# The output stage of a decoder block by seven products: another order of the products, sums stored from ScalarE's queue, no arithmetic on GpSimd

## The chip, the cores and the metric

The kernel runs on one core of one Trainium2 chip. The time is that of the whole program on the device, in microseconds. A core has TensorE (PE, matmul), VectorE (DVE), ScalarE (ACT), GpSimd (POOL) and SyncE (SP). Each engine runs its own instructions in the order in which they are written for it, and waits on semaphores for the others. SP, ACT and POOL also start DMAs from their queues.

## The reference, cut to what matters

A block of a decoder: a norm, one projection of the input, differential attention and a gated linear recurrence (RG-LRU) side by side, an output projection added to the residual, and a last norm. The change lies in the last three lines:

```python
h = rmsnorm(x, norm_g[l], NORM_EPS)
proj = einsum('btd,de->bte', h, w_in[l])        # q, k, v, g_att, u, g_lru
att = diff_attention(...) * silu(g_att)         # (1, T, 1024)
rec = rg_lru_branch(u, ...) * silu(g_lru)       # (1, T, 1024)
mixed = concatenate([att, rec], axis=-1)        # (1, T, 2048)
x = x + einsum('bte,ed->btd', mixed, w_out[l])  # w_out is 2048 x 2048
return rmsnorm(x, final_g, NORM_EPS)[:, N_META:]   # 1024 rows of 2048
```

## The kernel before

Every float32 product is made from two parts of each operand: `split` (L79, L80) writes a high part on ACT (`whi`, or half of a `mix` tile) and the rest on DVE (`wlo`). Each product takes three matmuls, high x high (L684), high x low (L685) and low x high (L686).

The last stage, `out_proj`, computes mixed @ w_out by seven products of half the size in each direction instead of eight, in the manner of Strassen and Winograd. The rows are two halves of 512: A is half 0 of mixed (transposed, 16 pieces `mix_d[0][e]` of 128x512 in DRAM), B half 1. Pieces 0 to 7 are the attention part, 8 to 15 the recurrent part. The left factors are A's first pieces (for w11), A's second (w21), s1 = B first + B second (t1), s2 = s1 - A first, s3 = A first - B first, s4 = A second - s2, and x22 = B second. The right factors are the blocks w11, w21, w22 of w_out and the sums t1 = w12 - w11, t2 = w22 - t1, t3 = w22 - w12, t4 = t2 - w21. The name on the left in `plan` is the right factor of a product; the second name is the left factor that is *loaded during it* (`left_factor`), and used by the next product (during w11 nothing is loaded, since the second half of the 16 pieces is there already). So before, the products are w11 x A first, w21 x A second, t1 x s1, w22 x s4, t2 x s2, t3 x s3, t4 x x22.

A product is two passes (`pair`), one for each half of its 1024 columns, and sums over 1024, with four accumulators of 128 rows x 512 columns in a pass. A pass takes four weight tiles of 128x1024 (`ep`), each good for 24 matmuls. For a weight tile `right_factor` loads `wraw` from SP's queue (two buffers), for t1 to t4 also `wb` (three buffers), subtracts on DVE (L658), stores the sums t1 and t2 to DRAM (L661, `t_d`) for the later products that need them, and splits into `whi` and `wlo` (three buffers each). Behind the weight tile's loads (`issue_after`) come those of one piece of the next left factor: `mix`, and where it is a sum also `xb` (four buffers), a subtraction or addition on DVE (L635), for s2 a second one (L640) and a store (L641), and a split. The second pass of the last product loads all its weights ahead (`wlast`) and goes row tile by row tile.

At a pass's end the accumulators are added into `y` (L700) by what `sinks` lists; "x" adds the residual x (L697). A last contribution to a quarter of a row tile is squared and summed on ACT (L704) and, if it is not the last quarter, multiplied by g, the last norm's weight (L706). After four quarters `finish` computes the row's factor (L717 to L721), scales the four quarters (ACT and DVE, L727, L730, L731) and stores the rows (L733).

The stage before it is the recurrent branch for half 1 (`lruB`). Its projections take weight tiles of w_in from SP's queue, and in blocks 1 to 4 `load_mix` fetches and splits A's 16 pieces for the first product.

A scheduler places the instructions: each engine's order follows from what it expects of times, not from the order in the code alone, so the lists of both kernels are compared below.

## Time and profile before

| | us |
|---|---|
| median of 3 runs (lowest, highest) | 1640.6 (1637.65, 1643.15) |
| the profiled execution, its own time | 1637.0 |
| its span in the trace | 1635.2 |
| output stage, first to last matmul | about 1308 to 1626 |

The profiled execution is one run, somewhat shorter than the median. Busy times are sums over the span. A time in a list of an engine's instructions is the start, in us from the span's start, then the duration; "[1.11 <-DVE wlo L80]" says that the engine was idle for 1.11 us before it and that the end of DVE's wlo released it. A queue's issuing of DMAs (SPq, ACTq, POOLq) isn't counted as busy. The stretches that the rows below are cut into are the products: w21 is 1352 to 1396, t1 1396 to 1447, w22 1447 to 1491, and t4 1578 to 1627.

### The profile page before, as it was taken

How to read it: one execution, taken by the hardware profiler on the slowest of the kernel's cores; microseconds unless marked ns; L12 is line 12 of the kernel's file. 1: busy time of each engine (PE TensorE's matmuls, PEld its weight loads, DVE VectorE, ACT ScalarE, POOL GpSimd, SP SyncE). 2: the span in 40 equal slices, each digit the busy share in tenths (PEclk: the TensorE clock that was granted, in tenths of full speed). 3: DMA queues.
4: the chain of work that ended last, by engine and by line, in shares of the span. 5: the costliest groups of instructions: out<-in, count | busy, mean ns of one | idle time of the engine just before them, and what ended most of it. 6: DMA issues, size and time to landing. Idle time of an engine off the chain costs nothing.

```text
span 1635.2 us, 22985 instructions
## 1 busy us (share of the span) xinstructions
PE 1596.9 (98%) x8466; PEld 1370.8 (84%) x8466; DVE 1117.6 (68%) x2218; ACT 874.1 (53%) x1392; POOL 205.2 (13%) x308
## 2 busy tenths in 40 slices
PE   7999999999999999999999999999999999899996
PEld 6889889998989888888888888887887887788885
DVE  6766556665676667667668667757877656867996
ACT  5655555545566657456556556545776543332533
POOL 1211111110011010201011001000000002200262
PEclk9999999999999999999999999999999999999999
DMA  9633344333344443533234234233443388969874
GB/s 310 206 121 109 116 137 132 122 124 108 122 146 145 145 142 123 183 114 116 84 120 134 78 120 123 78 97 100 138 138 114 120 309 290 326 234 330 307 283 154
DMA packets 85196, 261.61 MB, mean 160 GB/s; under 512 B 11659, under 2 KB 13748, under 8 KB 84956
## 3 DMA queue, kind: packets, MB, share of 16 engines
q1 hardware_dynamic: 60544, 192.18, 35.2%
q0 software_dynamic: 24304, 67.90, 12.6%
q8 instruction: 67, 1.10, 0.3%
q14 instruction: 45, 0.37, 0.1%
q10 hardware_dynamic: 236, 0.06, 0.0%
HBM read 213.35 MB, written 39.86 MB: 155 GB/s over the span
## 4 chain that ended last, share of the span: by engine, by line
PE 75%; DVE 8%; issue 7%; DMA 7%; ACT 3%; POOL 1%; SPq 0%; ACTq 0%; DVEq 0%; POOLq 0%
PE proj L158 20%; PE proj L159 19%; PE proj L160 19%; PE T L396 2%; PE o L685 2%; PE o L686 2%; PE o L684 2%; DVE wlo L80 2%; PE S L341 2%; PE S L339 2%; DMA wb<-w_out 1%; DVE y L700 1%; DVE wb L658 1%; DMA xb<-mix_d 1%; DMA xt<-x 1%
## 5 line engine op out<-in xcount | busy, mean ns | idle before, releaser
L158 PE MATMUL proj<-hTA,whi 128*128 128x256 f32 (+2 forms) x1152 | 373.5, 325 | 1.9 <-ACT whi L79 1.9
L159 PE MATMUL proj<-hTA,whi 128*128 128x256 f32 (+2 forms) x1152 | 370.4, 322 | 0.0
L160 PE MATMUL proj<-hTA,wlo 128*128 128x256 f32 (+2 forms) x1152 | 369.5, 322 | 0.5 <-DVE wlo L80 0.5
L79 ACT ACTIVATE whi<-wraw 128x1024 fp32r<-128x1024 f32 (+1 forms) x218 | 228.2, 1047 | 244.8 <-PE proj L159 186.6
L80 DVE TENSOR_TENSOR wlo<-wraw,whi 128x1024 fp32r<-128x1024 f32 (+1 forms) x218 | 264.0, 1212 | 116.5 <-ACT whi L79 116.3
L158 PE MATMUL proj<-hTB,whi 128*128 128x512 f32 x768 | 302.1, 393 | 1.2 <-DVE gr L291 0.6
L160 PE MATMUL proj<-hTB,wlo 128*128 128x512 f32 x768 | 300.9, 392 | 0.0
L159 PE MATMUL proj<-hTB,whi 128*128 128x512 f32 x768 | 299.8, 390 | 0.0
L158 PEld LDWEIGHTS proj<-hTA,whi 128*128 128x128 f32 x1152 | 218.8, 190 | 18.7 <-ACT whi L79 2.6
L160 PEld LDWEIGHTS proj<-hTA,wlo 128*128 128x128 f32 x1152 | 218.7, 190 | 16.3 <-DVE wlo L80 0.7
L159 PEld LDWEIGHTS proj<-hTA,whi 128*128 128x128 f32 x1152 | 219.0, 190 | 14.4
L685 PE MATMUL o<-wlo,mix 128*128 128x512 f32 x416 | 163.2, 392 | 7.9 <-DVE wlo L80 7.9
L158 PEld LDWEIGHTS proj<-hTB,whi 128*128 128x128 f32 x768 | 144.3, 188 | 30.4 <-DVE gr L291 2.6
L160 PEld LDWEIGHTS proj<-hTB,wlo 128*128 128x128 f32 x768 | 144.2, 188 | 30.1
L159 PEld LDWEIGHTS proj<-hTB,whi 128*128 128x128 f32 x768 | 144.3, 188 | 28.6
L686 PE MATMUL o<-whi,mix 128*128 128x512 f32 x416 | 162.6, 391 | 0.0
L684 PE MATMUL o<-whi,mix 128*128 128x512 f32 x416 | 162.5, 391 | 0.0
L358 ACT ACTIVATE s<-s,st 128x144 f32<-128x144 f32 (+7 forms) x128 | 100.0, 782 | 50.9 <-DVE st L356 50.1
L685 PEld LDWEIGHTS o<-wlo,mix 128*128 128x128 f32 x416 | 78.4, 189 | 26.4 <-DVE wlo L80 10.0
L351 DVE TENSOR_SCALAR_CACHE_REDUCE s<-S,b 128x256 f32<-128x256 f32 (+5 forms) x176 | 82.6, 477 | 19.4 <-PE S L341 16.2
L684 PEld LDWEIGHTS o<-whi,mix 128*128 128x128 f32 x416 | 78.5, 189 | 16.6 <-ACT gate L488 0.3
L686 PEld LDWEIGHTS o<-whi,mix 128*128 128x128 f32 x416 | 78.5, 189 | 16.2
(240 smaller groups left out, 2357.6 us busy)
## 6 DMA issues: line engine op xcount, KB each, us to landing
wraw<-w_in SPq DMA_DIRECT2D x190, 512.0 KB, 4.0
wraw<-w_out SPq DMA_DIRECT2D x48, 512.0 KB, 4.3
mix<-mix_d SPq DMA_DIRECT2D x48, 256.0 KB, 5.1
wb<-w_out SPq DMA_DIRECT2D x24, 512.0 KB, 5.1
t_d<-wb POOLq DMA_DIRECT2D x16, 512.0 KB, 6.8
xb<-mix_d SPq DMA_DIRECT2D x24, 256.0 KB, 6.4
kk_d<-kk POOLq DMA_DIRECT2D x8, 528.0 KB, 3.0
kk<-kk_d POOLq DMA_DIRECT2D x8, 528.0 KB, 4.1
```

The costliest lines, as they stand in the source:

```text
L79: nc.scalar.activation(hi, src, AF.Copy)
L80: nc.vector.tensor_tensor(out=lo, in0=src, in1=hi.bitcast(F32), op=ALU.subtract)
L158: nc.tensor.matmul(ps[:, :n], lhsT=hi[:, c], rhs=xh, start=(kt == 0), stop=False)
L159: nc.tensor.matmul(ps[:, :n], lhsT=hi[:, c], rhs=xl, start=False, stop=False)
L160: nc.tensor.matmul(ps[:, :n], lhsT=lo[:, c], rhs=xh, start=False, stop=(kt == KT - 1))
L339: nc.tensor.matmul(ps[:, :w], lhsT=qq[:, j, qc], rhs=kk[:, j, c0:c0 + w], start=True, stop=False)
L341: nc.tensor.matmul(ps[:, :w], lhsT=self.qz[:, j, qc], rhs=kl[:, c0:c0 + w], start=False, stop=True)
L351: nc.vector.tensor_scalar(out=s[j][:, a:a + n], in0=ps[:, a - c0:a - c0 + n], scalar1=self.b31[:, h:h + 1], scalar2=-3.0e38, op0=ALU.add, ...
L358: nc.scalar.activation(s[j][:, :s_len], s[j][:, :s_len], AF.Exp, bias=nm[:, j:j + 1], accum_out=l[:, j:j + 1])
L684: nc.tensor.matmul(acc, lhsT=x[:, 0, tk], rhs=w[0], start=start, stop=False)
L685: nc.tensor.matmul(acc, lhsT=x[:, 0, tk], rhs=w[1], start=False, stop=False)
L686: nc.tensor.matmul(acc, lhsT=x[:, 1, tk], rhs=w[0], start=False, stop=stop)
```

## The change

Five things are done in `out_proj` and what feeds it.

1. The products' order. After: w11 x A first, w21 x A second, t1 x s1, t2 x s2, t3 x s3, t4 x x22, w22 x s4. So rows of half 1 get their last contribution in t4, and those of half 0 in w22; half 1 is finished during w22's first pass.
2. s3 is computed early: `load_mix` loads B's piece (`x3`, two buffers) beside A's, subtracts on DVE (L627 of the kernel after) and stores the difference in DRAM (`s3_d`) from POOL's queue; the output stage loads it as one piece.
3. The stores of s2, t1 and t2 are issued from ACT's queue, not POOL's.
4. POOL computes nothing: x is added by DVE, and for half 0 the product with g is DVE's too. For half 1 there is none; its `finish` scales all four quarters with one DVE operation each that takes the row's factor and g together.
5. The output rows of half 1 are stored from POOL's queue and those of half 0 from SP's, the other way round than before.

```diff
@@ -614,10 +614,19 @@
 
 
 
-    def load_mix(self, pool, half, e):
+    def load_mix(self, pool, stage, e):
+
+        nc = self.nc
+        A, B = self.mix_d
         t = pool.tile([P, 2, HALF], F32R, tag="mix", name="mix", bufs=16)
-        self.nc.sync.dma_start(out=t[:, 1].bitcast(F32), in_=self.mix_d[half][e])
-        self.split(t[:, 0], t[:, 1], t[:, 1].bitcast(F32))
+        x = t[:, 1].bitcast(F32)
+        nc.sync.dma_start(out=x, in_=A[e])
+        if e < 8:
+            b = stage.tile([P, HALF], F32, tag="x3", name="x3", bufs=2)
+            nc.sync.dma_start(out=b, in_=B[e])
+            nc.vector.tensor_tensor(out=b, in0=x, in1=b, op=ALU.subtract)
+            nc.gpsimd.dma_start(out=self.s3_d[e], in_=b)
+        self.split(t[:, 0], t[:, 1], x)
         return t
 
     def left_factor(self, name, pool, stage, e):
@@ -625,7 +634,7 @@
         nc = self.nc
         A, B = self.mix_d
         src = {"s1": (B[e], B[8 + e]), "s4": (A[8 + e], self.s2_d[e]), "s2": (self.s2_d[e], None),
-               "s3": (A[e], B[e]), "x22": (B[8 + e], None)}[name]
+               "s3": (self.s3_d[e], None), "x22": (B[8 + e], None)}[name]
         t = pool.tile([P, 2, HALF], F32R, tag="mix", name="mix", bufs=16)
         x = t[:, 1].bitcast(F32)
         nc.sync.dma_start(out=x, in_=src[0])
@@ -638,7 +647,7 @@
             b = stage.tile([P, HALF], F32, tag="xb", name="xb", bufs=4)
             nc.sync.dma_start(out=b, in_=A[e])
             nc.vector.tensor_tensor(out=b, in0=x, in1=b, op=ALU.subtract)
-            nc.gpsimd.dma_start(out=self.s2_d[e], in_=b)
+            nc.scalar.dma_start(out=self.s2_d[e], in_=b)
         self.split(t[:, 0], t[:, 1], x)
         return t
 
@@ -658,7 +667,7 @@
             nc.vector.tensor_tensor(out=b, in0=raw, in1=b, op=ALU.subtract)
             raw = b
         if src[2] is not None:
-            nc.gpsimd.dma_start(out=src[2], in_=raw)
+            nc.scalar.dma_start(out=src[2], in_=raw)
         if home is None:
             hi = self.wpool.tile([P, 1024], F32R, tag="whi", name="whi", bufs=3)
             lo = self.wpool.tile([P, 1024], F32R, tag="wlo", name="wlo", bufs=3)
@@ -691,27 +700,26 @@
             c = slice(cg * 512, (cg + 1) * 512)
             if kind == "copy":
                 nc.scalar.activation(y[:, c], acc, AF.Copy)
-            elif kind == "x":
-                b = stage.tile([P, HALF], F32, tag="xb", name="xr", bufs=4)
-                nc.sync.dma_start(out=b, in_=self.x[half * HALF + t * P:half * HALF + (t + 1) * P, c])
-                nc.gpsimd.tensor_tensor(out=y[:, c], in0=y[:, c], in1=b, op=ALU.add)
             else:
+                if kind == "x":
+                    acc = stage.tile([P, HALF], F32, tag="xb", name="xr", bufs=4)
+                    nc.sync.dma_start(out=acc, in_=self.x[half * HALF + t * P:half * HALF + (t + 1) * P, c])
                 other = ys[1][t][:, (cg & 2) * 512:(cg & 2) * 512 + 512] if kind == "left" else acc
                 nc.vector.tensor_tensor(out=y[:, c], in0=y[:, c], in1=other, op=ALU.subtract if kind == "sub" else ALU.add)
             if not final:
                 return
             n = done[half, t] = done.get((half, t), -1) + 1
             nc.scalar.activation(acc, y[:, c], AF.Square, accum_out=s[:, n:n + 1])
-            if n < 3:
-                nc.gpsimd.tensor_tensor(out=y[:, c], in0=y[:, c], in1=self.g_b[:, c], op=ALU.mult)
+            if n < 3 and not half:
+                nc.vector.tensor_tensor(out=y[:, c], in0=y[:, c], in1=self.g_b[:, c], op=ALU.mult)
             if n == 2:
                 nc.vector.tensor_reduce(out=s[:, 4:5], in_=s[:, 0:3], axis=AX.X, op=ALU.add)
                 nc.vector.tensor_scalar(out=s[:, 4:5], in0=s[:, 4:5], scalar1=1.0 / D, scalar2=EPS,
                                         op0=ALU.mult, op1=ALU.add)
             if n == 3:
-                finish(half, t, cg)
-
-        def finish(half, t, last):
+                finish(half, t)
+
+        def finish(half, t):
             y, s = ys[half][t], ss[half][t]
             r, v, n, m = s[:, 5:6], s[:, 3:4], s[:, 6:7], s[:, 7:8]
             nc.scalar.activation(r, v, AF.Sqrt, bias=s[:, 4:5], scale=1.0 / D)
@@ -721,28 +729,26 @@
             nc.vector.scalar_tensor_tensor(out=m, in0=n, scalar=3.0, in1=r, op0=ALU.subtract, op1=ALU.mult)
             row = slice(half * HALF + t * P, half * HALF + (t + 1) * P)
             for q in range(2):
-                c = [slice(512 * cg, 512 * cg + 512) for cg in ((2, 3) if last == 3 else (3, 2))] if q else \
-                    [slice(0, 512), slice(512, 1024)]
-                if q:
-                    nc.vector.scalar_tensor_tensor(out=y[:, c[1]], in0=y[:, c[1]], scalar=m, in1=self.g_b[:, c[1]],
-                                                   op0=ALU.mult, op1=ALU.mult)
-                else:
-                    nc.vector.tensor_scalar(out=y[:, c[1]], in0=y[:, c[1]], scalar1=m, scalar2=None, op0=ALU.mult)
-                nc.scalar.activation(y[:, c[0]], y[:, c[0]], AF.Copy, scale=m)
+                for i in range(2):
+                    c = slice(1024 * q + 512 * i, 1024 * q + 512 * (i + 1))
+                    if half or 2 * q + i == 3:
+                        nc.vector.scalar_tensor_tensor(out=y[:, c], in0=y[:, c], scalar=m, in1=self.g_b[:, c],
+                                                       op0=ALU.mult, op1=ALU.mult)
+                    elif i:
+                        nc.vector.tensor_scalar(out=y[:, c], in0=y[:, c], scalar1=m, scalar2=None, op0=ALU.mult)
+                    else:
+                        nc.scalar.activation(y[:, c], y[:, c], AF.Copy, scale=m)
                 c = slice(1024 * q, 1024 * (q + 1))
-                (nc.sync if half else nc.gpsimd).dma_start(out=self.out[row, c], in_=y[:, c])
-
-        def tiles():
-            return [self.ps.tile([P, 512], F32, tag="o", name="o", bufs=8) for _ in range(4)]
+                (nc.gpsimd if half else nc.sync).dma_start(out=self.out[row, c], in_=y[:, c])
 
 
         plan = [("w11", None, [("add", 0, 0, 0), ("copy", 1, 0, 0)]),
                 ("w21", "s1", [("add", 0, 0, 1)]),
-                ("t1", "s4", [("add", 0, 1, 0), ("add", 1, 1, 0)]),
-                ("w22", "s2", [("add", 0, 1, 0)]),
-                ("t2", "s3", [("add", 1, 0, 0), ("left", 0, 1, 1)]),
-                ("t3", "x22", [("add", 1, 0, 0), ("left", 1, 1, 1), ("x", 1, 0, 0)]),
-                ("t4", None, [("sub", 1, 0, 1)])]
+                ("t1", "s2", [("add", 0, 1, 0), ("add", 1, 1, 0)]),
+                ("t2", "s3", [("add", 1, 0, 0), ("left", 0, 1, 0)]),
+                ("t3", "x22", [("add", 1, 0, 0), ("left", 1, 1, 1)]),
+                ("t4", "s4", [("sub", 1, 0, 0)]),
+                ("w22", None, [("add", 0, 1, 1)])]
         x, x_next = mix[:8], mix[8:]
         for k, (right, left, sinks) in enumerate(plan):
             ahead = []
@@ -768,6 +774,9 @@
                         if k == 0 and pair == 1 and ep == 0:
                             nc.sync.dma_start(out=self.g_b, in_=self.final_g.partition_broadcast(P))
                             nc.vector.tensor_scalar(out=self.g_b, in0=self.g_b, scalar1=-0.5, scalar2=None, op0=ALU.mult)
+                        if k == 6:
+                            for cg in (0, 2):
+                                sink("x", None, 1, ep, cg, 1)
                         if left:
                             ahead.append(self.left_factor(left, xpool, stage, 4 * pair + ep))
                     for i in range(2):
@@ -791,6 +800,7 @@
         self.kl_d = [dram.tile([P, LA], F32, name=f"kl_d{h}") for h in range(H)]
         self.v_d = [dram.tile([P, 2, 4, P], F32, name=f"v_d{h}") for h in range(H)]
         self.vm_d = [dram.tile([MR, P], F32, name=f"vm_d{h}") for h in range(H)]
+        self.s3_d = [dram.tile([P, HALF], F32, name=f"s3_d{e}") for e in range(8)]
         self.s2_d = [dram.tile([P, HALF], F32, name=f"s2_d{e}") for e in range(8)]
         self.t1_d = [[dram.tile([P, 1024], F32, name=f"t1_d{p}_{i}") for i in range(4)] for p in range(2)]
         self.t2_d = [[dram.tile([P, 1024], F32, name=f"t2_d{p}_{i}") for i in range(4)] for p in range(2)]
@@ -880,7 +890,7 @@
                     if 1 <= b < 5:
                         with tc.issue_after(self.last_w.ins):
                             for _ in range(2):
-                                mixA.append(self.load_mix(m1, 0, len(mixA)))
+                                mixA.append(self.load_mix(m1, pool, len(mixA)))
         tail.close()
         right.close()
         ps_cm.__exit__(None, None, None)
```

ScalarE during w21, in both kernels. `mix` is the split of a piece of s1, `whi` that of a weight tile, and `s2_d` the store of s2's piece (s_d in the trace). Before:

```order
L79 ACTIVATE mix_12973<-xb_12975 128x512
L79 ACTIVATE whi_12968<-wraw_12966 128x1024
L79 ACTIVATE mix_13031<-xb_13033 128x512
L79 ACTIVATE whi_13026<-wraw_13024 128x1024
L79 ACTIVATE mix_13073<-xb_13075 128x512
L79 ACTIVATE whi_13068<-wraw_13066 128x1024
```

After:

```order
L79 ACTIVATE mix_13013<-xb_13015 128x512
L650 DMA s2_d3_106<-xb_13018 128x512
L79 ACTIVATE whi_13008<-wraw_13006 128x1024
L79 ACTIVATE mix_13071<-xb_13073 128x512
L650 DMA s2_d4_107<-xb_13076 128x512
L79 ACTIVATE whi_13066<-wraw_13064 128x1024
L79 ACTIVATE mix_13113<-xb_13115 128x512
L650 DMA s2_d5_108<-xb_13118 128x512
L79 ACTIVATE whi_13108<-wraw_13106 128x1024
```

A store now stands between the split of a piece and that of the weight tile behind it.

VectorE late in the last product but one tile. Before, this is the second half of t4, where `wb` are the differences and `wlast` the last pass's low parts:

```order
L80 TENSOR_TENSOR wlo_14696<-wb_14692,whi_14695 128x1024
L658 TENSOR_TENSOR wb_14725<-wraw_14723,wb_14725 128x1024
L700 TENSOR_TENSOR y1_3_12553<-y1_3_12553 128x512
L658 TENSOR_TENSOR wb_14782<-wraw_14780,wb_14782 128x1024
L80 TENSOR_TENSOR wlo_14729<-wb_14725,whi_14728 128x1024
L658 TENSOR_TENSOR wb_14791<-wraw_14789,wb_14791 128x1024
L80 TENSOR_TENSOR wlast_14786<-wb_14782,wlast_14785 128x1024
L80 TENSOR_TENSOR wlast_14795<-wb_14791,wlast_14794 128x1024
```

After, it is w22's first pass, where `y1_0` to `y1_2` are row tiles of half 1 (each "x4" is four quarters) and `wlo_14724` is that pass's fourth weight tile:

```order
L729 SCALAR_TENSOR_TENSOR ss1_2_12600<-ss1_2_12600 128x1
L735 SCALAR_TENSOR_TENSOR y1_0_12590<-y1_0_12590,ss1_0_12598,fg_b_12585 128x512 x4
L735 SCALAR_TENSOR_TENSOR y1_1_12591<-y1_1_12591,ss1_1_12599,fg_b_12585 128x512 x4
L735 SCALAR_TENSOR_TENSOR y1_2_12592<-y1_2_12592,ss1_2_12600,fg_b_12585 128x512 x4
L80 TENSOR_TENSOR wlo_14724<-wraw_14721,whi_14723 128x1024
L80 TENSOR_TENSOR wlast_14799<-wraw_14796,wlast_14798 128x1024
```

The differences are gone from there, and twelve full scalings of half 1 stand ahead of the split that the first pass's fourth weight tile needs.

SyncE in the recurrent stage, after; before, there are only the `mix` and `wraw` loads:

```order
L118 DMA wraw_11506<-w_in 128x1024
L623 DMA mix_11595<-mix_d0_4_131 128x512
L623 DMA mix_11603<-mix_d0_5_132 128x512
L626 DMA x3_11480<-mix_d1_2_145 128x512
L118 DMA wraw_11611<-w_in 128x1024
L626 DMA x3_11488<-mix_d1_3_146 128x512
L118 DMA wraw_11617<-w_in 128x1024
L623 DMA mix_11679<-mix_d0_6_133 128x512
L626 DMA x3_11597<-mix_d1_4_147 128x512
L623 DMA mix_11687<-mix_d0_7_134 128x512
L118 DMA wraw_11701<-w_in 128x1024
```

The loads of `x3` stand among those of w_in's weight tiles.

## Rows read from the trace of the kernel before

**Rows 1.** The page's first part: busy us (share of the span) and instructions.

```profile
PE 1596.9 (98%) x8466; PEld 1370.8 (84%) x8466; DVE 1117.6 (68%) x2218; ACT 874.1 (53%) x1392; POOL 205.2 (13%) x308
```

**Rows 2.** Stretches: length, busy us (count) PE PEld DVE ACT POOL, clock, DMA, GB/s.

```profile
1352.00:1396.00 44.00, 41.81 (x183) 33.95 (x182) 29.89 (x36) 15.36 (x27) 10.78 (x11) 1.00 0.84 289
1396.00:1447.00 51.00, 47.66 (x203) 38.65 (x202) 39.98 (x46) 17.43 (x27) 10.56 (x11) 0.97 0.97 348
1447.00:1491.00 44.00, 44.00 (x196) 36.45 (x195) 27.74 (x34) 14.08 (x17) 1.60 (x3) 1.00 0.62 205
...
1578.00:1627.00 49.00, 44.27 (x193) 35.67 (x191) 39.49 (x55) 19.30 (x38) 20.31 (x13) 1.00 0.45 157
```

**Rows 3.** Timeline of PE: start, duration, instruction [idle before, what ended it].

```profile
1351.98 0.39 PE L684 MATMUL o<-whi,mix 128*128 128x512 f32 x1
...
1386.12 0.50 PE L685 MATMUL o<-wlo,mix 128*128 128x512 f32 x1 [1.11 <-DVE wlo L80]
...
1392.96 0.50 PE L685 MATMUL o<-wlo,mix 128*128 128x512 f32 x1 [1.08 <-DVE wlo L80]
...
1400.22 0.50 PE L685 MATMUL o<-wlo,mix 128*128 128x512 f32 x1 [1.49 <-DVE wlo L80]
...
1413.26 0.50 PE L685 MATMUL o<-wlo,mix 128*128 128x512 f32 x1 [1.86 <-DVE wlo L80]
...
1597.07 0.50 PE L685 MATMUL o<-wlo,mix 128*128 128x512 f32 x1 [2.40 <-DVE wlo L80]
...
1607.29 0.50 PE L685 MATMUL o<-wlast,mix 128*128 128x512 f32 x1 [1.76 <-DVE wlast L80]
```

**Rows 4.** Timeline of DVE in w21: subtractions for pieces of the left factor.

```profile
1373.00 0.69 DVE L640 TENSOR_TENSOR xb<-xb 128x512 f32<-128x512 f32 x1
...
1379.99 0.69 DVE L635 TENSOR_TENSOR xb<-mix,xb 128x512 f32<-128x512 f32 x1 [4.16 <-DMA xb<-mix_d]
```

**Rows 5.** The page's DMA issues: count, size, median us from issue to landing.

```profile
xb<-mix_d SPq DMA_DIRECT2D x24, 256.0 KB, 6.4
```

**Rows 6.** Timelines of DVE (two splits) and POOL in t4.

```profile
1578.42 1.23 DVE L80 TENSOR_TENSOR wlo<-wb,whi 128x1024 fp32r<-128x1024 f32 x1 [1.21 <-ACT whi L79]
...
1594.73 2.28 DVE L80 TENSOR_TENSOR wlo<-wb,whi 128x1024 fp32r<-128x1024 f32 x1
...
1593.69 2.24 POOL L697 TENSOR_TENSOR y<-y,xr 128x512 f32<-128x512 f32 x1
```

**Rows 7.** DVE from 1300 by line and shape: busy us, mean ns | idle before.

```profile
L658 DVE TENSOR_TENSOR wb<-wraw,wb 128x1024 f32<-128x1024 f32 x32 | 46.5, 1453 | 17.6 <-DMA wb<-w_out 8.5 <-DMA wraw<-w_out 5.8 <-DMA wb<-t_d 3.3
L700 DVE TENSOR_TENSOR y<-y,o 128x512 f32<-128x512 f32 x64 | 41.1, 680 | 4.4 <-PE o L686 4.4
L80 DVE TENSOR_TENSOR wlo<-wb,whi 128x1024 fp32r<-128x1024 f32 x28 | 40.0, 1428 | 3.2 <-ACT whi L79 3.2
...
L727 DVE SCALAR_TENSOR_TENSOR y<-y,ss,fg_b 128x512 f32<-128x512 f32 x8 | 6.0, 744 | 0.0
...
L718 DVE TENSOR_SCALAR ss<-ss 128x1 f32<-128x1 f32 x8 | 1.7, 209 | 4.5 <-ACT ss L717 4.5
```

**Rows 8.** Timeline of DVE in t1: a difference that waits for its operand.

```profile
1407.96 1.23 DVE L658 TENSOR_TENSOR wb<-wraw,wb 128x1024 f32<-128x1024 f32 x1 [3.72 <-DMA wb<-w_out]
```

**Rows 9.** Timeline of ACT's queue at the start: DMA issues.

```profile
0.75 0.41 ACTq L808 DMA_DIRECT2D g_col<-norm_g  x1
...
1.67 0.63 ACTq L550 DMA_DIRECT2D oh<-onehot  x1
```

**Rows 10.** The recurrent stage: SP's mix loads, a PE wait, POOL's small stores (issues).

```profile
1162.00 0.90 SPq L619 DMA_DIRECT2D mix<-mix_d  x2
...
1175.80 0.86 SPq L619 DMA_DIRECT2D mix<-mix_d  x2
...
1237.83 0.50 PE L485 MATMUL S<-uh,lwh 128*128 128x512 f32 x1 [1.05 <-ACT uh L79]
...
s_d<-xb POOLq DMA_DIRECT2D x8, 256.0 KB, 4.1
```

## The prediction, made before the changed kernel was run

> **What bounds the kernel now.** I read the busy shares first. TensorE (PE) computes for 98% of the span, VectorE (DVE) for 68% [rows 1]: an edit can win only what PE loses by waiting or at a lower clock, and costs something only where PE is made to wait. The stretches of the output stage show next where that is [rows 2]: the 44 us from 1447 (w22) are full of PE, the two stretches before it (w21 and t1) and the last one (t4) are not. PE's timeline then names the waits [rows 3]: two in the last tiles of w21 (1386.12, 1392.96), two in the first three tiles of t1 (1400.22, 1413.26), two in t4 (1597.07, 1607.29). Each ends with a wlo or wlast, the low part that DVE splits off a weight tile. The six idle times are 1.11, 1.08, 1.49, 1.86, 2.40 and 1.76 us, and each of these matmuls takes 0.50 us where the one at 1351.98 takes 0.39 [rows 3], 0.11 more. From 1396 to 1447 the granted clock is 0.97 [rows 2], which is 51 x 0.03 = 1.5 us lost at the lower level after the waits. So:
>
> - w21 and t1: 5.54 idle + 4 x 0.11 + 1.5 = **7.5 us**.
> - t4: 4.16 + 2 x 0.11 = **4.4 us**.
>
> Nothing else of size can be won in the stage that the change rewrites.
>
> The two groups have different causes. In w21 and t1 the supply is late. SyncE's (SP's) queue issues the operands of a left factor behind the weight tile; DVE sits 4.16 us until one has landed and takes it only then [rows 4]; such a load needs a median 6.4 us from issue to landing [rows 5], while the stretches move 289 and 348 GB/s against 205 in w22 [rows 2]. In t4 DVE itself is slow: the wlo split that takes 1.23 us at 1578.42 takes 2.28 at 1594.73, beside a tensor_tensor of GpSimd (POOL) that begins at 1593.69 and lasts 2.24 [rows 6].
>
> **The change part by part.** The sum is made against the profiled execution, 1637.0 us, of which 1635.2 is its span. The median of the three runs is 1640.6, so 3.6 us are added at the end.
>
> *POOL's arithmetic goes.* POOL does 24 products with g and eight additions of x like the one at 1593.69 [rows 6]. After, DVE does 12 of the products (half 0 only) and the eight additions at 0.68, and twelve more scalar_tensor_tensor at 0.744 that fold g into the end of half 1: 20 x 0.68 + 12 x 0.744 = 22.5 us more [rows 7] (the four tensor_scalar that half 1 no longer has are not counted). Against this stand eight subtractions for s3 that leave the stage, at 0.69 [rows 4] 5.5 us, and the slowing beside POOL: 28 splits at a mean 1428 ns and 32 differences at 1453 [rows 7] against the undisturbed 1.23 us [rows 6], 28 x 0.20 + 32 x 0.22 = 12.6. DVE's total grows by 4.4 us, and DVE is not the bound. What counts is the place: t4's two waits are DVE at half speed beside POOL. With POOL idle they go, **-4.4 us**; if other DVE work in t4 is half of the cause, -2.2.
>
> *w22 comes last.* Its weight tiles need one load and no difference, so the last two passes have the lightest supply. But half 1 is finished in w22's first pass, all on DVE. In the order, when t4's last accumulators are complete (time T) DVE runs eight additions, the third tile's wlo, some 14 small operations, then twelve scalar_tensor_tensor and only then the fourth tile's wlo: 8 x 0.68 + 1.23 + 14 x 0.2 + 12 x 0.744 + 1.23 = 19.6 us [rows 6, 7] (0.2 for a small one, as the mean of eight on 128x1 [rows 7]). PE comes to that tile three tiles after T. A tile is 44 / 8 = 5.5 us of a full stretch [rows 2], 24 matmuls; eight matmuls that don't need this wlo stand in front, 1.8 us: T + 18.3. That is a wait of 1.3, or less by up to 0.8 as DVE starts when the first accumulator closes, before T. I take **+1.0**, ends 0 and +4 (the burst also stands behind x loads, 6.4 us like others of their size [rows 5], of which about half could show). The end behind PE's last matmul has the same operations on the other half's rows: 0.
>
> *The four waits in w21 and t1.* Two edits pull at them. (a) The stores of s2, t1 and t2 (24) go from POOL's queue, where nothing urgent stood behind them, to ScalarE's (ACT's). There a store stands ahead of the next whi split in five tiles of w21 and in t1 and t2. Behind it wait whi, then wlo on DVE, then PE. A DMA issue takes ACT 0.41 to 0.63 us [rows 9], and the store must first wait for the second subtraction, 0.69 [rows 4]: 0.4 to 1.3 for one link, and I take 0.7, nearer the low end because ACT splits mix meanwhile. The loop of the supply, whose margin is gone by the end of w21, gets longer by it: +1.7 over the four waits, ends 0 and +2.8 (0.7 on each). (b) During t1 the change prefetches s2, one load per tile, where s4 needed two: 8 x 256 KB = 2.1 MB less of the 51 x 348 GB/s = 17.7 MB of that stretch [rows 2], 12%. If landing times shrink by 12%, a load lands 0.8 us earlier [rows 5], half of t1's waits of 1.49 and 1.86. Worth -1.7, a third of what lies there, ends 0 and -5.1 (both waits, 2 x 0.11 and the clock's 1.5). Together **0**, ends -5.1 and +2.8.
>
> Nobody waits for these stores soon, so their own speed wins nothing. The Trainium skill ("DMA: Bandwidth & Descriptors", section "Issuing engines are not separate DMA queues") speaks against this move in a wider way: transfers started by ScalarE, SyncE or GpSimd run on the same 16 engines and interleave, and a further starting engine saves only sequencer time. By it the sum stays at 1638.2; were ACT's queue a path of its own beside SP's, the stores would leave the loads alone and rival A's 1633.1 would follow. No large store starts from ACT in the trace of before.
>
> *s3 in the recurrent stage.* Eight loads x3, eight DVE subtractions and eight stores on POOL are put into the stage ahead. x3 has two buffers, so in SP's queue the third x3 load waits for a store: load 6.4, subtraction 0.7, issue at most 0.63, landing 4.1 = 11.8 us [rows 4, 5, 9, 10]. The pairs of mix loads come 13.8 us apart there (1162.00, 1175.80) [rows 10], so the cycle just fits. But weight tiles of w_in stand behind those loads, and PE already waits 1.05 us for that stage's work at 1237.83 [rows 10]. **+1.0**, ends 0 and +4.1 (one store's landing, once).
>
> Sum: 1637.0 - 4.4 + 1.0 + 0 + 1.0 = 1634.6; plus 3.6: **1638.2 us**. With one or two terms at an end this case reaches from 1634 to 1642.
>
> **The rivals.** A measurement of this kernel tells about 0.3% (4.9 us) from no change: faster is below 1635.7, slower above 1645.5.
>
> *A, the supply relaxes.* 2.1 MB less let t1's loads land early enough; its two waits and the lower clock go as well: 1638.2 - 5.1 = **1633.1**, faster. For it: the waits lie in the two stretches with the most traffic before w22, and the clock fell only after them. Against it: w21's own traffic is the same, and it is w21 that hands t1 an empty margin.
>
> *B, ACT's queue ties supply and differences together: slower.* Before, w22 stood between t1 and t2, and PE ran it without a wait at 205 GB/s [rows 2]: the margin was refilled. After, t1, t2, t3 and t4 follow each other, all with two loads and a difference, and in t1 and t2 ACT holds a split back until the store behind that difference is issued. DVE already sits 3.72 us for the second operand there (1407.96) [rows 8]. The point from which it decides: the loop from one weight tile to the next takes longer than PE's 5.5 us. If it is longer by 0.4, about half of the link's 0.7, the 16 tiles of t1 and t2 and six of t3 lose 22 x 0.4 = 8.8: **1647.0**. Against it: DVE is no longer slowed, and the store's wait adds delay to a tile but not work to an engine.
>
> *C, it only changes place.* The burst in w22 takes its upper end, or the x3 chain its own: 3 to 4 us more, **1642**, no change that can be told.
>
> **How the numbers follow.** Forecast 0.42, A 0.32, B 0.12, C 0.14. Faster: A nearly whole (0.30) and the low edge of the forecast (0.06), 0.36; slower: B, 0.12; within 0.3%: the rest, 0.52. The range leaves out B and the ends of A and C: 1630 (A with w21's two waits gone as well, another 2.4) to 1644 (C with 2 us more).
>
> **What would show it.** Right: PE without a wait on wlo or wlast in t4; POOL without any tensor_tensor and the differences at 1.23 us; one wait of 0.5 to 1.5 us at the fourth weight tile of w22, ended by DVE; waits still at the end of w21. A shows as a clock of 1.00 and no idle PE in t1. B shows as PE waits in t1 and t2 with whi late and a store ahead of it on ACT. Wrong altogether: the recurrent stage longer by over 4 us, or waits where I see none, between t2 and t3.

## The result and the profile after

The changed kernel takes 1649.25 us (median of 11 runs, 1644.46 to 1652.74) against 1639.39 for the kernel before: ratio 1.0064, 95% interval 1.0050 to 1.0079. It is slower by some 10 us. One of the 11 runs of the kernel before took 1979.69 us, far from the other ten, and is not in the ratio. The forecast was 1638.2, no change that can be told, with a range of 1630 to 1644, and the time lies above it.

The page's first part of the kernel after, as [rows 1]:

```profile
span 1647.2 us, 22990 instructions
## 1 busy us (share of the span) xinstructions
PE 1599.7 (97%) x8466; PEld 1370.0 (83%) x8466; DVE 1111.8 (67%) x2246; ACT 868.3 (53%) x1384; POOL 140.7 (9%) x260
```

The span grew by 12.0 us (1635.2 to 1647.2). PE's busy time grew by 2.8, so most of the 12 us are waits. POOL is busy for 64 us less (the rows count its own issuing of a DMA, some 0.53 us, as busy) and DVE for 6 us less, and no engine has become the bound by its busy time.

The stretches of the output stage after, as [rows 2] (length, busy us of PE, PEld, DVE, ACT and POOL, granted clock, DMA share, GB/s; PEld is TensorE's loading of weights). In the new order they are w21, t1, t2, t3, t4 and w22:

```profile
1356.00:1402.80 46.80, 44.32 (x195) 35.95 (x193) 30.36 (x42) 17.56 (x28) 0.00 (x0) 1.00 0.81 285
1402.80:1449.00 46.20, 44.43 (x194) 35.82 (x193) 33.80 (x40) 14.80 (x23) 0.00 (x0) 1.00 0.91 332
1449.00:1494.00 45.00, 43.81 (x193) 35.95 (x192) 34.88 (x42) 14.69 (x18) 0.00 (x0) 1.00 0.88 314
1494.00:1544.70 50.70, 44.80 (x194) 35.75 (x193) 34.91 (x43) 13.86 (x22) 0.00 (x0) 1.00 0.67 228
1544.70:1594.50 49.80, 44.99 (x194) 35.64 (x193) 34.01 (x49) 17.37 (x29) 0.00 (x0) 1.00 0.62 206
1594.50:1638.00 43.50, 43.50 (x193) 35.84 (x191) 35.41 (x83) 18.69 (x42) 4.27 (x8) 1.00 0.55 201
```

t3 and t4 are the long ones, 50.7 and 49.8 us where a full product takes 43.5. They are also stretches with little traffic (228 and 206 GB/s against 332 in t1): what is late there is not bandwidth. DVE is busy for 34 to 35 us of some 50, so it is not short of time either.

PE's waits in t3 and t4 (start, duration, instruction, idle before and what ended it), as [rows 3]; two of over 1 us and two of 0.3 are left out:

```profile
1500.86 0.50 PE L694 MATMUL o<-wlo,mix 128*128 128x512 f32 x1 [1.00 <-DVE wlo L80]
...
1525.45 0.50 PE L694 MATMUL o<-wlo,mix 128*128 128x512 f32 x1 [0.79 <-DVE wlo L80]
1533.89 0.50 PE L694 MATMUL o<-wlo,mix 128*128 128x512 f32 x1 [2.71 <-DVE wlo L80]
...
1577.76 0.50 PE L694 MATMUL o<-wlo,mix 128*128 128x512 f32 x1 [2.34 <-DVE wlo L80]
```

Now what DVE and SP's queue do ahead of the two waits in the middle. The first fence is DVE's timeline, the second SP's and a row of ACT's:

```profile
1516.44 1.22 DVE L80 TENSOR_TENSOR wlo<-wb,whi 128x1024 fp32r<-128x1024 f32 x1
1517.58 0.68 DVE L80 TENSOR_TENSOR mix<-mix 128x512 fp32r<-128x512 f32 x1
1523.03 1.22 DVE L667 TENSOR_TENSOR wb<-wraw,wb 128x1024 f32<-128x1024 f32 x1 [4.78 <-DMA wb<-w_out]
1524.18 1.22 DVE L80 TENSOR_TENSOR wlo<-wb,whi 128x1024 fp32r<-128x1024 f32 x1
...
1530.87 1.23 DVE L667 TENSOR_TENSOR wb<-wraw,wb 128x1024 f32<-128x1024 f32 x1 [1.28 <-DMA wb<-w_out]
...
1532.61 1.22 DVE L80 TENSOR_TENSOR wlo<-wb,whi 128x1024 fp32r<-128x1024 f32 x1
```

```profile
1517.68 0.33 SPq L666 DMA_DIRECT2D wb<-w_out  x1
...
1525.42 0.33 SPq L666 DMA_DIRECT2D wb<-w_out  x1
...
1533.86 0.33 SPq L666 DMA_DIRECT2D wb<-w_out  x1
...
1516.36 1.04 ACT L79 ACTIVATE whi<-wb 128x1024 fp32r<-128x1024 f32 x1
```

Read them crosswise. A low part ends at 1517.66, and 0.02 us later SP issues a load of wb: the end of that low part set a buffer free. (In t3 and t4 SP waited for the end of a low part ahead of 13 loads of wb.) DVE's next weight instruction is the difference for the load just issued, and it waits 4.78 us for it. Only behind it stands the next low part (1524.18), which PE needs at 1525.45 and whose operands had been ready since whi's end (1516.36 + 1.04 = 1517.40). Its end lets the next load go (1525.42), and so on. From one low part to the next it takes 7.7 and 8.4 us, where PE uses up a tile in 5.44. The chain that ended last runs through the same links from 1516 to 1532: low part, load (5.27 us), difference, low part, load (5.43 us), difference.

In numbers of tiles: by the scheduler's order the difference of tile n+2 stands ahead of the low part of tile n. With three buffers the load for tile n+2 can start only when tile n-1's low part is done. So a whole load lies between the low parts of n-1 and n. I call this a **lead of two**: two tiles whose low part still stands behind a difference. Before, in t3, the lead was one:

```profile
1532.59 1.22 DVE L80 TENSOR_TENSOR wlo<-wb,whi 128x1024 fp32r<-128x1024 f32 x1
...
1533.84 0.33 SPq L657 DMA_DIRECT2D wb<-w_out  x1
...
1541.59 1.20 DVE L658 TENSOR_TENSOR wb<-wraw,wb 128x1024 f32<-128x1024 f32 x1
...
1549.06 1.22 DVE L80 TENSOR_TENSOR wlo<-wb,whi 128x1024 fp32r<-128x1024 f32 x1
```

(DVE, SP and DVE twice, of the kernel before.) The load goes at 1533.84 behind the low part of t3's second tile, and DVE takes its difference, that of the fifth tile, at 1541.59 without waiting. This tile's own low part comes at 1549.06, behind those of two other tiles. The loop spans three tiles in 16.5 us, 5.5 for one.

The lead can be read from the order that the scheduler gives DVE, without any run. The table has one digit for each of a product's eight differences, the number of earlier tiles whose low part still stands behind it. Beside it is what the product lost: the time from its first matmul to that of the next product (for t4 of before, the last one, to its last matmul), less eight tiles of 5.44 us, from PE's timeline. A loss holds PE's idle time and what matmuls took longer behind it: 5.9 of t3's 7.12 us and 4.6 of t4's 6.30 are idle time.

| kernel | t1 | t2 | t3 | t4 | lost: w21, t1, t2, t3, t4 (us) |
|---|---|---|---|---|---|
| before | 01111111 | 11111111 | 11111111 | 00001101 | 2.85, 5.54, 0, 0, 4.79 |
| after | 11111111 | 11111111 | 11222122 | 21222122 | 3.14, 2.69, 1.53, 7.12, 6.30 |

The profiled span's 12.0 us are then: 0.9 up to PE's last wait of about 1 us in the attention (at 1133.01 before, 1133.90 after), 3.2 from there to the output stage's first matmul, which I call the recurrent stage (1308.33 before, 1312.46 after), 7.6 in the output stage (20.8 lost against 13.2) and 0.3 behind the last matmul.

### The profile page after: what moved, and what is told of

Read it like the earlier page. It is cut to its first block, busy times and chain, and to the rows that moved or that the text cites. A ratio compares the mean times of both kernels' runs of the same rounds, so it can differ in the third digit from the quotient of the medians.

```text
span 1647.2 us, 22990 instructions
## 1 busy us (share of the span) xinstructions
PE 1599.7 (97%) x8466; PEld 1370.0 (83%) x8466; DVE 1111.8 (67%) x2246; ACT 868.3 (53%) x1384; POOL 140.7 (9%) x260
## 4 chain that ended last, share of the span: by engine, by line
PE 70%; DMA 11%; DVE 9%; issue 5%; ACT 4%; POOL 1%; SPq 0%; ACTq 0%; DVEq 0%; POOLq 0%
PE proj L158 18%; PE proj L159 18%; PE proj L160 18%; DMA wb<-w_out 3%; PE o L694 2%; PE o L693 2%; PE o L695 2%; DVE wlo L80 2%; PE T L396 2%; DMA wraw<-w_in 2%; PE S L341 2%; PE S L339 2%; DVE y L708 1%; ACT whi L79 1%; DMA mix<-s_d 1%
## 5 line engine op out<-in xcount | busy, mean ns | idle before, releaser
L79 ACT ACTIVATE whi<-wraw 128x1024 fp32r<-128x1024 f32 (+1 forms) x214 | 224.1, 1047 | 238.9 <-PE proj L159 184.7
L80 DVE TENSOR_TENSOR wlo<-wraw,whi 128x1024 fp32r<-128x1024 f32 (+1 forms) x214 | 259.2, 1212 | 113.7 <-ACT whi L79 111.3
L694 PE MATMUL o<-wlo,mix 128*128 128x512 f32 x416 | 163.6, 393 | 16.2 <-DVE wlo L80 16.0
```

What stands on the lines that cost most here:

```text
L79: nc.scalar.activation(hi, src, AF.Copy)
L80: nc.vector.tensor_tensor(out=lo, in0=src, in1=hi.bitcast(F32), op=ALU.subtract)
L694: nc.tensor.matmul(acc, lhsT=x[:, 0, tk], rhs=w[1], start=False, stop=False)
```

## The experiments

The three theories of the expectations are L (the lead), Q (the ScalarE queue, rival B of the prediction) and M (the margin that w22 no longer refills). Every kernel was timed against the kernel before on the same chip.

**The stores back on GpSimd's queue.**

```diff
-            nc.scalar.dma_start(out=self.s2_d[e], in_=b)
+            nc.gpsimd.dma_start(out=self.s2_d[e], in_=b)
...
-            nc.scalar.dma_start(out=src[2], in_=raw)
+            nc.gpsimd.dma_start(out=src[2], in_=raw)
```

> The changed kernel with one part undone: the stores of s2, t1 and t2 go from GpSimd's queue again, not ScalarE's. The order on VectorE stays as it is. Theory L (the lead): the new waits stand in t3 and t4, where no sum is stored, because VectorE there makes a weight tile's difference two tiles ahead of the low part it has to split, while only three buffers hold the second operand; each tile then waits for a whole load. By it this kernel still takes 1647 to 1651 us, with over 11 us of waits in t3 and t4. Theory Q (the rival that I had put on record as B: ScalarE's queue ties stores and splits together): the waits go, 1637 to 1642 us.

Measured: 1649.27 us, ratio 1.0061 (1.0041 to 1.0080). That is the changed kernel's time. The leads are the same as in the changed kernel, and the products lose 3.81, 2.61, 1.57, 6.95 and 4.73 us. Q falls: which queue issues these stores makes no difference that can be told, neither a cost nor a gain.

**A lead of at most one.** An edge in the issue order is all that is added, with no wait and no work:

```diff
-            nc.vector.tensor_tensor(out=b, in0=raw, in1=b, op=ALU.subtract)
+            with self.tc.issue_after(self.los[-2].ins):
+                nc.vector.tensor_tensor(out=b, in0=raw, in1=b, op=ALU.subtract)
...
+        self.los.append(self.last_lo)
```

`los` lists the low parts of the weight tiles, so `los[-2]` at tile n is the low part of tile n-2.

> The changed kernel with one constraint on the order: VectorE may make the difference of weight tile n only behind the low part of tile n-2, so it runs at most one tile ahead. Theory L: t3 and t4 lose 13 us now and about 3 after, so some 10 us less, 1638 to 1641 us. Theory Q, and a theory M (the margin was refilled by w22 between t1 and t2, and without it the supply by 228 GB/s is too slow at any order): within 2 us of 1649.

Measured: 1636.01 us, ratio 0.9980 (0.9966 to 0.9994), 13.2 us less than the changed kernel. t3 and t4 lose nothing (w21 5.27, t1 2.14, t2 1.42). The stretches t3 and t4 of this kernel:

```profile
1494.00:1537.50 43.50, 43.50 (x193) 36.03 (x192) 37.03 (x45) 15.34 (x24) 0.00 (x0) 1.00 0.81 277
1537.50:1581.00 43.50, 43.50 (x193) 36.03 (x193) 32.52 (x47) 16.03 (x27) 0.00 (x0) 1.00 0.61 213
```

PE is busy for all of both, with the same work on every engine and at as little traffic in t4. Its order of products is the new one, so M falls as well: the margin refills without w22 between. (In the changed kernel the low part of t3's first tile ends 0.1 us before PE begins that tile; here t3's eight low parts end 2.6 to 7.3 us before.) The idle time of DVE ahead of the differences, 43.7 us after, is 22.4 here. For DVE in t3 the rows now read:

```profile
1508.87 1.23 DVE L80 TENSOR_TENSOR wlo<-wb,whi 128x1024 fp32r<-128x1024 f32 x1 [0.26 <-ACT whi L79]
1510.35 1.23 DVE L668 TENSOR_TENSOR wb<-wraw,wb 128x1024 f32<-128x1024 f32 x1 [0.25 <-DMA wb<-w_out]
1511.58 0.69 DVE L80 TENSOR_TENSOR mix<-mix 128x512 fp32r<-128x512 f32 x1
1512.53 1.23 DVE L80 TENSOR_TENSOR wlo<-wb,whi 128x1024 fp32r<-128x1024 f32 x1 [0.25 <-ACT whi L79]
```

Difference and low part alternate 3.7 us apart, and DVE's wait for the load is 0.25 us.

**Four buffers for wb.**

```diff
-            b = stage.tile([P, 1024], F32, tag="wb", name="wb", bufs=3)
+            b = stage.tile([P, 1024], F32, tag="wb", name="wb", bufs=4)
```

> The changed kernel with four buffers for the second operand of a difference where it has three. The scheduler then lets VectorE run two to three tiles ahead in t3 and t4. Theory L says that what counts is the lead against the buffers: with a lead of two and four buffers a load has 5.4 us more, so the waits fall by half or more, 1641 to 1645 us; where the lead is three the loop of one tile is back. Theory Q and M: no more than 2 us change, since neither the stores nor the traffic differ.

Measured: 1638.33 us, ratio 0.9986 (0.9971 to 1.0001). The leads grow with the buffers, t3 22223223 and t4 33232323. t3 loses 4.58 and t4 2.10, half of the 13.4 us of the changed kernel. It is better than expected because w21 and t1 lose almost nothing (0.00 and 0.52). L is right about t3 and t4 together, but not about the place: t4 has the more threes and loses less. So a lead of three with four buffers did not cost what a lead of two costs with three. Why a fourth buffer helps w21, which has no differences of its own, L does not say.

**A lead of two forced on the kernel before, in t3 alone.** The program's text makes the difference of tile n+2 first and puts the split of tile n behind it:

```diff
-                    ws = self.right_factor(right, pair, ep, stage, None)
+                    n = 4 * pair + ep
+                    if k == 5:
+                        while len(diffs) < min(n + 3, 8):
+                            diffs.append(self.right_factor(right, len(diffs) // 4, len(diffs) % 4, stage, None, True))
+                        self.last_w = diffs[n][2]
+                        with self.tc.issue_after(diffs[min(n + 2, 7)][1].ins):
+                            ws = self.halves(diffs[n][0], None)
+                    else:
+                        ws = self.right_factor(right, pair, ep, stage, None)
```

(`halves` is the part of `right_factor` that splits, now called by itself.)

> The kernel before with one thing added: in t3 VectorE must make the difference of weight tile n+2 ahead of the low part of tile n (a lead of two, as the changed kernel has it in t3 and t4); order of products, stores and GpSimd's arithmetic stay. Theory L: a loop of one tile takes a load of some 5.3 us, a difference of 1.2 and a low part of 1.2, 7.7 us against PE's 5.44, so six tiles lose up to 2.3 us each less the 4 to 6 us of margin that t3 starts with: 4 to 10 us more in t3 and the start of t4, 1643 to 1649 us. Theory M (it was w22's place that mattered): no change, 1638 to 1641.

Measured: 1656.89 us, ratio 1.0094 (1.0078 to 1.0110). The leads in t3 are 11222222, and t3 loses 22.1 us where it lost nothing: 16.2 of them idle time, the rest at a granted clock of 0.90 over the product, where t3 had 1.00. The sign is L's, and M falls again; the size is more than twice what I expected. PE's two longest waits there, and DVE ahead of the second one:

```profile
1562.42 0.50 PE L688 MATMUL o<-wlo,mix 128*128 128x512 f32 x1 [3.91 <-DVE wlo L80]
...
1578.54 0.79 PE L688 MATMUL o<-wlo,mix 128*128 128x512 f32 x1 [9.64 <-DVE wlo L80]
```

```profile
1566.69 0.69 DVE L703 TENSOR_TENSOR y<-y,o 128x512 f32<-128x512 f32 x1 [3.06 <-PE o L689]
...
1574.00 2.28 DVE L658 TENSOR_TENSOR wb<-wraw,wb 128x1024 f32<-128x1024 f32 x1
1576.20 2.28 DVE L80 TENSOR_TENSOR wlo<-wb,whi 128x1024 fp32r<-128x1024 f32 x1
```

Ahead of the difference DVE also had the additions of the finished pass, which waited 3.06 us for PE's last matmul, and the difference and the low part then took 2.28 us each, as beside GpSimd in [rows 6] (its additions and products run here from 1568.92 to 1582.55). So DVE waited for PE, and PE for DVE: the 7.7 us were only the load's part of the loop.

**The new order of products alone, on the kernel before.**

```diff
-                ("t1", "s4", [("add", 0, 1, 0), ("add", 1, 1, 0)]),
-                ("w22", "s2", [("add", 0, 1, 0)]),
...
+                ("t1", "s2", [("add", 0, 1, 0), ("add", 1, 1, 0)]),
...
+                ("w22", None, [("add", 0, 1, 1)])]
```

> The kernel before with one part of the change alone: the new order of products (and the queues of the two halves' output rows); GpSimd's arithmetic, its stores and s3 in the output stage stay. In the scheduler's order the lead is one in t1 and t2, mostly one in t3 and mixed, one and two, in t4. Theory L: next to nothing lost in t2 and t3, 3 to 7 us in t4, 1638 to 1645 us. Theory M (without w22 between t1 and t2 the margin is never refilled): waits in t2 and t3 too, 4 us or more in each, over 1646.

Measured: 1644.95 us, ratio 1.0026 (1.0015 to 1.0038). Leads 00111121 in t3 and 21212112 in t4; lost 4.83, 6.44, 1.02, 0.32 and 6.21, and 2.03 in w22. The losses of t2, t3 and t4 are what L expected, and M's waits of 4 us or more in t2 and t3 are not there. But t4 lost 4.79 us before as well, with GpSimd's arithmetic beside it, which is here too; its 6.21 alone don't show what the leads cost. Two things follow. The new order by itself is slower by some 5 us. In the profiled runs its output stage takes 7.7 us more than before: 2.9 in w21 and t1, 1.0 in t2, 0.3 in t3, 1.4 in t4 and 2.0 in w22. So the leads of two, in t4, can account for a small part of it only; where the rest comes from is not shown. And t1 loses 6.44 us here although it loads as little as in the changed kernel: the smaller traffic alone does not shorten t1's waits.

**GpSimd's arithmetic alone moved, on the kernel before.**

```diff
-                nc.gpsimd.tensor_tensor(out=y[:, c], in0=y[:, c], in1=b, op=ALU.add)
+                nc.vector.tensor_tensor(out=y[:, c], in0=y[:, c], in1=b, op=ALU.add)
...
-                nc.gpsimd.tensor_tensor(out=y[:, c], in0=y[:, c], in1=self.g_b[:, c], op=ALU.mult)
+                nc.vector.tensor_tensor(out=y[:, c], in0=y[:, c], in1=self.g_b[:, c], op=ALU.mult)
```

> The kernel before with one part of the change alone: GpSimd's 24 products with g and eight additions of x go to VectorE. If t4's two waits are VectorE at half speed beside GpSimd, as I had forecast, the 4.8 us of t4 go: 1633 to 1636 us. If VectorE's own load in t3 and t4 is what is late (22 us more work there), t4 keeps its waits: 1638 to 1643.

Measured: 1631.31 us, ratio 0.9947 (0.9934 to 0.9960), below the range that was expected. t4's loss goes from 4.79 to 0; w21 and t1 keep theirs (2.43 and 5.71). No lead is above one, before or here. t4 of this kernel, where [rows 2] has 44.27 us of PE in 49.00:

```profile
1578.00:1621.70 43.70, 43.70 (x194) 36.01 (x192) 34.55 (x64) 18.36 (x37) 0.00 (x0) 1.00 0.44 154
```

DVE is busy for less of it than before, 34.55 us against 39.49 in [rows 2], although work was added to it.

**s3 back in the output stage.** The five lines of `load_mix` from `if e < 8` on that make s3 are taken out, and

```diff
-               "s3": (self.s3_d[e], None)
+               "s3": (A[e], B[e])
```

> The changed kernel without s3's early computation: the recurrent stage loads and stores nothing for it, and the output stage loads both pieces and subtracts, as before. If the x3 loads in SyncE's queue hold back the weights of the recurrent stage, the output stage starts 4 us earlier (its first matmul at about 1308 instead of 1312); the eight loads and subtractions come back in t2, where they may cost up to 3. Expected 1645 to 1648 us. If the recurrent stage's 4 us have another cause, its first matmul stays at 1312.

Measured: 1637.91 us, ratio 0.9993 (0.9979 to 1.0008), 11 us less than the changed kernel and far more than expected. The recurrent stage takes 175.4 us as before (175.3); in the changed kernel it takes 178.6. The other 8 us I had not foreseen: with s3's loads and subtractions back in t2, the scheduler's leads in t3 became 10111112 and t3 lost nothing, while t4's stayed 21222122 and lost 5.32. An edit in the product before had changed the lead in t3, and the time went with it. So of the changed kernel's two products with leads of two, t4 has them from the new order alone, and t3 only with s3 early as well. To have the two effects apart, both edits together:

> The changed kernel with s3 computed in the output stage and a lead of at most one, three buffers. Both effects measured apart: 2.7 us less in the recurrent stage, t3 and t4 without waits; w21 and t1 keep theirs. Theory L: 1632 to 1635 us. If the two gains overlap (a lead of one in t3 came with s3 alone already, and took 11 us): no better than 1636.

Measured: 1632.80 us, ratio 0.9964 (0.9951 to 0.9977). A lead of one and s3 in the output stage: 3.2 us better than the lead alone by the medians, 2.6 by the ratios, whose intervals overlap. The recurrent stage agrees, 175.3 us against 178.0. So early s3 costs about 3 us, and the rest of the 11 was the lead.

**What in the recurrent stage costs the 3 us.** Its rows after, as [rows 10] (PE's longest wait there, and ACT ahead of it):

```profile
1219.42 1.22 PE L485 MATMUL S<-uh,lwh 128*128 128x512 f32 x2 [2.73 <-ACT uh L79]
```

```profile
1206.30 0.63 ACT L79 ACTIVATE mix<-mix 128x512 fp32r<-128x512 f32 x1 [3.29 <-DMA mix<-mix_d]
...
1218.73 0.63 ACT L79 ACTIVATE uh<-uc 128x512 fp32r<-128x512 f32 x1 [0.33 <-DVE uc L470]
```

Two edits to the kernel with a lead of one, in the same two lines:

```diff
-            nc.sync.dma_start(out=b, in_=B[e])
+            nc.gpsimd.dma_start(out=b, in_=B[e])
             nc.vector.tensor_tensor(out=b, in0=x, in1=b, op=ALU.subtract)
```

> The changed kernel with a lead of at most one and the x3 loads issued from GpSimd's queue, not SyncE's; traffic, subtractions and stores of s3 stay. With x3 in SyncE's queue the recurrent stage took 2.7 us more than before (first matmul of the output stage 178.0 us after the last attention wait, 175.3 before). Theory X (a load that waits for s3's store holds the mix and weight loads behind it): the 2.7 us go, 1633 to 1634.5 us. Rival: VectorE's and the DMA's extra work there is the cause: no change, 1635.5 to 1637.

Measured: 1636.58 us, ratio 0.9981 (0.9970 to 0.9993). SP no longer waits for a store of s3 (10.5 us in four waits in the changed kernel), and the recurrent stage takes 178.8 us all the same. Theory X falls as far as SP's queue goes. The wait itself only moved: on GpSimd's queue two loads of x3 now wait 6.6 us for a store of s3, and a subtraction on DVE waits 2.9 us for such a load.

```diff
             nc.sync.dma_start(out=b, in_=B[e])
-            nc.vector.tensor_tensor(out=b, in0=x, in1=b, op=ALU.subtract)
```

> The changed kernel with a lead of at most one, and without the eight subtractions for s3 in the recurrent stage: the pieces of B are loaded and stored as they are (the subtraction is left out, so s3 is not the difference). Loads, stores and queues are those of the kernel with a lead of one. If VectorE's eight subtractions, 5.5 us in all, and their places in its order are what delays the recurrent stage, its 2.7 us go: 1633 to 1634 us, first matmul of the output stage 175 to 176 us after the last attention wait. If it is the 4 MB more of transfers, nothing changes: 178 us, 1635.5 to 1637.

Measured: 1637.47 us, ratio 0.9987 (0.9975 to 1.0000), and 181.6 us for the recurrent stage, longer than expected. The subtractions by themselves are not the cause either. But here SP waits again for stores of s3, 6.3 us in three waits, so each of the two edits left a link that the other took out, and none took out both. What is left is the wait for a store by two buffers of x3, the 4 MB of loads and stores, s3's stores in GpSimd's queue (all these kernels have them there), or another order of ACT's work that came with them. These runs don't tell them apart.

**Versions that beat both kernels.** The changed kernel with s3 in the output stage, four buffers and a lead of one:

> The changed kernel with s3 computed in the output stage, four buffers for the second operand and a lead of at most one. By the runs so far: the recurrent stage as before (4 us less than in the changed kernel), w21 and t1 without their waits as with four buffers (5 us less), t3 and t4 without waits (13 us less), something left in t2: 1649 - 22 = 1627, 1625 to 1631 us. If four buffers helped only by the longer lead, w21 and t1 keep their waits: 1632 to 1635.

Measured: 1629.51 us, ratio 0.9927 (0.9914 to 0.9941); lost 1.24, 0.42, 2.90, 0, 0. And the kernel before, in its own order of products, with GpSimd's arithmetic on DVE, four buffers and a lead of one:

> The kernel before, its order of products and queues kept, with GpSimd's arithmetic on VectorE, four buffers for the second operand and a lead of at most one. GpSimd's part alone gave 1631.3. If four buffers take away the waits of w21 and t1 in this order of products as in the other (8.1 us here), 1624 to 1627 us; if that hung on the new order or on ScalarE's stores, 1630 to 1632.

Measured: 1625.91 us, ratio 0.9914 (0.9900 to 0.9929); lost 0, 2.46, 0, 0, 0. This is the best of the kernels run, 23 us below the changed one. It keeps one of the change's parts only, GpSimd's arithmetic.

## Why the prediction was wrong, point by point

- **POOL's arithmetic, -4.4: right in t4, and too small as a whole.** The part alone takes t4's loss from 4.79 to 0, and the profiled runs differ by 4.7 us (1637.0 to 1632.3). By the ratio of all runs it is worth 8.7 us (6.6 to 10.8); where the other 4 lie, no trace shows. DVE's total in the stage, forecast to grow by 4.4 us, fell by 11.3 (240.7 to 229.4), among others because the sum had counted the slowing beside POOL for weight tiles only. In the kernel after, the differences take a mean 1224 ns where [rows 7] has 1453, and POOL does nothing in the output stage but issue the stores of the output rows. The rows for that stage, DVE's first (count, busy us and mean ns, idle before and releasers):

```profile
L667 DVE TENSOR_TENSOR wb<-wraw,wb 128x1024 f32<-128x1024 f32 x32 | 39.2, 1224 | 43.7 <-DMA wb<-w_out 27.2 <-DMA wb<-t_d 7.5 <-DMA wraw<-w_out 5.5
L80 DVE TENSOR_TENSOR wlo<-wb,whi 128x1024 fp32r<-128x1024 f32 x32 | 39.0, 1220 | 3.1 <-ACT whi L79 3.1
```

```profile
L742 POOL DMA_DIRECT2D out<-y x8 | 4.3, 534 | 288.8 <-DVE y L735 288.8
```

The first row also holds the failure. DVE stood idle for 43.7 us ahead of the differences, where [rows 7] has 17.6. Time saved on DVE was spent in waiting for loads.

- **The burst in w22, +1.0: its lower end, 0.** The fourth tile's low part ended at 1611.05, 0.24 us after PE began that tile at 1610.81, and the eight matmuls put in front covered it. The order was read rightly, the burst reckoned too long: from PE's first matmul of w22 (1594.5) to the end of that low part it took 16.6 us where the sum has 19.6.

- **The stores on ACT, +1.7: 0.** With the stores back on GpSimd's queue nothing moved by more than the runs differ (1649.27 against 1649.25). The Trainium skill's rule that I had set beside it ("DMA: Bandwidth & Descriptors", "Issuing engines are not separate DMA queues") agrees with these runs: 0.02 us between the two queues.

- **Less traffic in t1, -1.7: not settled.** w21 and t1 together lost 5.83 us after, 8.39 before. That lies between the ends I gave, but the new order alone, with the same loads in t1, lost 11.3 there, so the smaller traffic does not by itself shorten the waits.

- **s3 early, +1.0: mis-sized.** It cost 3.2 us in the changed kernel's recurrent stage, inside the ends of 0 and 4.1. That it comes from SP's queue, held up behind a store, is not borne out: with the loads of x3 out of that queue the stage took as long. The cause is open.

- **The step that failed** is the one I didn't make: "nothing else of size can be won in the stage that the change rewrites", and with it no term for new waits in t2, t3 and t4, because PE ran in t2 and t3 without waits before and t4's were to go. The three have 15.0 us of loss after, where they had 4.8. The path that was left out is DVE's own order: in t3 and t4 the differences stand two tiles ahead of the low parts, with three buffers of wb, so that a whole load of 5.3 to 5.4 us lies between two low parts and a tile takes 7.7 to 8.4 us where PE needs 5.44. Held at a lead of one, t3 and t4 lose nothing, and the kernel takes 1636.0 us instead of 1649.25. I had put on record "waits where I see none, between t2 and t3" as what would make it wrong altogether. The waits in t3 and t4 are in that class.

- **Rival B had the size, 1647.0, for the wrong reason.** It put the loss into the loop between weight tiles, longer than PE's 5.5 us, and there it was. But neither of its two causes, ACT's stores and w22's absence, is the one. With the stores back on GpSimd's queue the time stayed, and with a lead of one the same order of products, without w22 between, ran t3 and t4 without a wait. That its number came near is luck. It speaks of "t1 and t2 and six of t3"; t1 and t2 lost little, and t4 most beside t3.

- **What could have been seen.** Both orders were there. I compared ACT in w21 and DVE in w22, where parts of the change stand, and not the place of the differences against the low parts in the four products that stayed. The leads of t3 and t4 are plain in those lists. Where a scheduler orders the work, an edit to the plan is an edit to all that it orders.

- **The rest of the sum** comes near when the lead is taken out: the changed kernel with a lead of one takes 1636.0, and the forecast was 1638.2 (1634 to 1642). That is in part luck. Against the trace of before, this kernel has -4.8 us in t4 (forecast -4.4), -1.0 in w21 and t1 together (0), +1.4 in t2 (no term), 0 from the burst (+1.0) and +2.7 in the recurrent stage (+1.0); the errors cancel.

## What to carry to other kernels

Where a producer (here the difference) and the consumer that sets its buffer free (the low part) run on one in-order engine, count how many tiles ahead the producer is queued and compare it with the number of buffers: at a lead of buffers less one, each tile waits for a whole load, at one less the load is hidden. That is shown here for three buffers; with four, leads of three cost less (2.1 us in t4). One place more took 13 us of 1640, and an edge in the issue order gave them back. After any change to what a scheduler orders, look for this in every loop that it touches, also where the kernel of before had no wait.

## What the runs showed that I had not expected

- The lead decides over more than bandwidth does: t3 and t4 lost 7.12 and 6.30 us at 228 and 206 GB/s, and w21, t1 and t2 of the same kernel 3.14, 2.69 and 1.53 at 285, 332 and 314.
- A fourth buffer for wb also shortened w21, in both orders of products: from 3.14 us of loss to 0.00 in the new one, from 4.51 to 1.24 there with a lead of one and s3 in the output stage, and from 2.43 to 0.00, together with a lead of one, in the order of before. w21 itself needs no differences of weight tiles. In the kernel after, the late low part of w21 (1390.17) stands on DVE behind a subtraction for s1 that waited 4.57 us for its load; with four buffers that wait is 1.64. Why the load comes sooner, no run here says.
- s3's early work, with eight loads and eight stores of 256 KB, cost the recurrent stage 2.7 to 4.8 us in the five kernels that kept all of it there, whichever queue issued the loads; leaving the subtractions out didn't help. In the changed kernel 1.9 of the 3.2 us are idle time of PE (3.9 us against 2.0 before); the granted clock behind its longest wait there is 0.94 (1220 to 1240), where it was 1.00.
